# Where the new recurrent states are computed in the second feed-forward, and how its chunk borders are ordered

## The chip, the cores and the metric

The kernel runs on one core of a Trainium2 chip. The metric is the device time of one execution in microseconds (us), lower is better. Engines are named as in the profile: PE is the matrix engine (PEld its weight load), DVE the vector engine, ACT the scalar engine, POOL the GpSimd engine (here it mostly issues DMAs), SP the sync engine, which issues the other DMAs. Each engine works through its own instructions in the order in which they stand; semaphores make one engine wait for another.

## The reference

One layer of a decoder for 512 new prompt tokens and 8 single tokens that continue older sequences, all in float32. Norms, scales and the other outputs are left out here.

```python
def _swiglu(x, wg, wu, wd):
    return (jax.nn.silu(x @ wg) * (x @ wu)) @ wd
...
h = h + 0.5 * _swiglu(_rms_norm(h, ffn1_norm[l]), ffn1_w_gate[l], ffn1_w_up[l], ffn1_w_down[l])
m, p, c, s = _hybrid_mixer(_rms_norm(h, mix_norm[l]), ...)
h = h + m
h = h + 0.5 * _swiglu(_rms_norm(h, ffn2_norm[l]), ffn2_w_gate[l], ffn2_w_up[l], ffn2_w_down[l])
...
# in the mixer, for each of the 8 continued sequences:
def step(h, inp):
    s, a = inp
    return a[..., None, None] * h + s, h
```

D_MODEL is 1024 and FFN_DIM 2816. The last piece gives, for each continued sequence, 16 heads and a 64 x 128 matrix per head, a new state: the old state times a decay plus the outer product of two short vectors. These new states are an output of their own (`nss`, 8 x 1024 x 128 numbers); nothing else in the kernel reads them.

## The kernel before

The tokens lie along the free dimension, 520 of them in two halves of 260, the features along the 128 partitions. A float32 product is made of three matmuls on rounded parts, `hi*hi + hi*lo + lo*hi` (`mm3`, lines 123 to 128), so each operand is split: ACT rounds it to `hi`, DVE computes `lo = x - hi`. For some weight pieces `lo` is made by ACT, which writes the negative of the rounded value, and by a DMA of POOL that adds the original onto it (lines 111 and 112).

The kernel has three stages: the first feed-forward, the mixer, the second feed-forward. Both feed-forwards are the class `Ffn`. Its hidden features are 22 tiles of 128, in chunks of 6, 6, 6 and 4 (`CHUNKS`). A tile `f` is one step, and after each of the first three chunks four more steps `(c, d)` with d = 0, 2, 4, 6 multiply what chunk c has made by the down weights and add it to `h`. Between them, the first tile of the next chunk is already stepped: the order at a border is last tile of the chunk, first tile of the next, then `(c, 0)`, `(c, 2)`, `(c, 4)`, `(c, 6)`. I call this place a chunk border; there are three in each feed-forward.

A step multiplies two pairs of blocks with seven products instead of eight (Strassen's scheme): `product(k, p)` for p in 1, 5, 6, 3, 7, 2, 4, where p = 4 is left for the step after (`flush`). Each p reads one of seven "slots", which are the two halves of the left and the right member of a pair of tiles and sums and differences of them. For the `(c, d)` steps these slots are made of the activations: `g_split` (lines 252 to 294) makes, from the pair's tiles `gx` and `out`, four combinations `xd`, and rounds and subtracts all seven into the tile `gt` (seven `hi`, seven `lo`). Product 1 reads slot 0, 5 reads slot 3, 6 slot 5, 3 slot 2, 7 slot 4, 2 slot 1, 4 slot 6. For a chunk's last pair a part is made early (`g_split(k, False)` from `gates`) and the rest when product 4 is done (`g_split(k, True)` from `close`). In the first feed-forward (`self.i == 1`) the last pair of a chunk is already treated in its own way: the third combination is computed from other inputs, slot 3 is rounded apart from slots 4 and 5, the gate's instructions get high priority (`first_if`), and the weights of product 4 are split after the others (`late` in `load`).

The new states are a generator, `new_states` (lines 1001 to 1043), which the second feed-forward advances: 32 units, each one sequence and two pairs of heads. A unit is advanced twice. The first advance issues on POOL the store of the previous unit's result (`out_nss`, line 1021) and the load of the next unit's old state (`hs`, line 1011; three buffers), and for every second unit a load of a row (`br`, line 1017). The second advance issues four ACT instructions (lines 1037 and 1038) and one DVE addition (`hs`, line 1039). All but the DVE addition are pinned to the program's order. Before, `step` advances the generator twice per step (lines 526 and 527), that is, one unit per step in every step until the 32 are done.

The instructions of each engine are put in order by a scheduler that simulates the program's time with costs of its own; the diff therefore moves instructions that it doesn't name.

Of the kernel before, what the change touches and what calls it, by code (L numbers as in the profile page):

```python
# [12 lines left out]
ALU = mybir.AluOpType  # L13
# [21 lines left out]
PAIRED = 3  # L35
# [26 lines left out]
def tile_trunk_step(ctx: ExitStack, tc: tile.TileContext, ins: dict, outs: dict):  # L62
    nc = tc.nc
# [38 lines left out]
    def split(src, n, name, hp, nb, tags, late=None):  # L102
        hi, lo = (hp.tile([P, 1024], F32R, tag=t, bufs=nb, name=f"{t}_{name}")[:, :n] for t in tags)
        h, l = hi, lo
        if len(src.shape) == 3:
            h, l = (t.rearrange("p (j c) -> p j c", j=src.shape[1]) for t in (hi, lo))
        cast = nc.scalar.copy(h, src)  # L107
        casts.append(cast.ins)
        q = 0 if late is None else n - late.shape[1]
        if late is not None:  # L110
            nc.scalar.activation(out=lo[:, q:], in_=src[:, q:], func=AF.Copy, scale=-1.0)
            nc.gpsimd.dma_start(out=lo[:, q:], in_=late, accum_op=ALU.add)
        if late is None or q:
            s = slice(0, q) if late is not None else slice(None)
            nc.vector.tensor_tensor(out=l[:, s], in0=src[:, s], in1=h[:, s].bitcast(F32), op=ALU.subtract)
        return hi, lo
# [92 lines left out]
    class Ffn:  # L209
# [42 lines left out]
        def g_split(self, f, late=None):  # L252
            role = self.role(f)
            if role == "plain" and late is not False:
                self.g_plain(f, self.out[f])
            if role != "second":
                return
            last = f == self.chunks[self.chunk[f]][-1]
            if not last and late is False:
                return  # L260
            gx, go = self.gx, self.out[f]
            if not last or late is not True:
                self.gt[f] = (self.gp.tile([P, 14, HB], F32R, tag="gt", bufs=3, name=f"gt{self.i}_{f}"),
                              self.gp.tile([P, 4, HB], F32, tag="xd", name=f"gd{self.i}_{f}"))
            t, xd = self.gt[f]

            def low(x, q):
                hi, lo = t[:, 0:7][:, q], t[:, 7:14][:, q]
                nc.scalar.copy(hi, x)
                nc.vector.tensor_tensor(out=lo, in0=x, in1=hi.bitcast(F32), op=ALU.subtract)  # L270

            if not last or late is not True:
                nc.vector.tensor_tensor(out=xd[:, 0], in0=gx[:, 0], in1=gx[:, 1], op=ALU.subtract)
                nc.vector.tensor_tensor(out=xd[:, 1], in0=go[:, 1], in1=gx[:, 1], op=ALU.subtract)
                x, y = (xd[:, 0], go[:, 1]) if self.i == 1 else (xd[:, 1], gx[:, 0])
                nc.vector.scalar_tensor_tensor(out=xd[:, 2], in0=x, scalar=-1.0, in1=y, op0=ALU.mult, op1=ALU.subtract)
                low(gx[:, 0], 0)
                if last:
                    if self.i == 1:
                        low(xd[:, 0], 3)  # L280
                        low(xd[:, 1:3], slice(4, 6))
                    else:
                        low(xd[:, 0:3], slice(3, 6))
                    low(go[:, 1], 2)
            if last and late is False:
                return
            nc.vector.scalar_tensor_tensor(out=xd[:, 3], in0=xd[:, 2], scalar=-1.0, in1=go[:, 0], op0=ALU.mult,
                                           op1=ALU.subtract)
            if last:
                low(go[:, 0], 1)  # L290
                low(xd[:, 3], 6)
            else:
                low(go, slice(1, 3))
                low(xd, slice(3, 7))
# [101 lines left out]
        def load(self, k):  # L396
            wx = self.wx
            n, src, nb, raw, f1, f2, add = self.added.pop(k) if k in self.added else self.sums(k)
            d1 = split(raw[:, 0, : 2 * nb], 2 * nb, f"{n}a", wp, 3, ("whi", "wlo"), src[0, :, nb:])
            if add is not None:  # L400
                add()
            late = self.i == 1
            if not late:
                d2 = split(raw[:, 1, nb : 2 * nb], nb, f"{n}b", wp, 3, ("whi", "wlo"), src[1, :, nb:])
            e1 = split(f1, 2 * nb, f"{n}c", wx, 2, ("shi", "slo"))
            e2 = split(f2, 2 * nb, f"{n}d", wx, 2, ("shi", "slo"))
            if late:
                with tc.issue_after(casts[-1]):
                    d2 = split(raw[:, 1, nb : 2 * nb], nb, f"{n}b", wp, 3, ("whi", "wlo"), src[1, :, nb:])
            m = nb // P  # L410
            self.w[k] = {1: (d1, 0), 2: (d1, m), 7: (e1, 0), 5: (e1, m), 6: (e2, 0), 3: (e2, m), 4: (d2, 0)}
# [60 lines left out]

        def first_if(self, k):
            c = self.chunk[k]
            return tc.high_priority() if self.i == 1 and c < PAIRED and k == self.chunks[c][-1] else nullcontext()

        def up(self, k, b, u):
            out, tg = self.out[k][:, b], self.tg[k][:, b]
# [20 lines left out]
        def rest(self, before, last_chunk):  # L499
            for c, fs in enumerate(self.chunks):  # L500
                last = c == len(self.chunks) - 1
                for f in fs[self.direct if c == 0 else 1 :] + ([] if last else self.chunks[c + 1][:1]):
                    self.step(f)
                    if last and self.gx is not None:
                        self.g_plain(fs[0], self.gx)
                        self.gx = None
                if not last:
                    for d in range(0, KD, 2):
                        self.step((c, d))
            self.product(self.pending, 4)  # L510
            with tc.high_priority():
                self.close(self.pending)
            wd = before()
            if wd is not None:
                self.down_by_half(c, min(fs), last_chunk, wd)
            else:
                self.down(c, min(fs), KF, last_chunk)

        def step(self, k):
            if k not in self.A:  # L520
                self.product(k, 1)
            self.flush()
            for p in (2, 5, 6, 3, 7) if k == KF - 1 else (5, 6, 3, 7, 2):
                self.product(k, p)
                if p == 3:
                    self.state()
            self.state()
            self.gates(k)
            self.pending = k

        def state(self):
            if self.states is not None:
                next(self.states, None)

        def down(self, c, lo, hi, after):
# [171 lines left out]
    todo, late = [], []  # L707
# [607 lines left out]
```

## Time and profile before

| | us |
|---|---|
| median of 3 runs | 978.83 |
| the 3 runs | 979.16, 973.38, 978.83 |
| the profiled execution, its own time | 969.87 |
| its span in the trace | 968.1 |

The profiled execution is 8.96 us below the median of the runs shown, and 1.77 us longer than its span. In this profile a matmul's start and the next one's start are about 0.12 us apart when nothing holds PE up, while each one's record is 0.28 us long, since matmuls overlap. An idle time printed in brackets counts from the end of the matmul before, so the time lost is read from the starts.

The stages of the second feed-forward, by what PE works on: the first chunk from 621 us, its border from about 670 to 692, the second border from 772 to 785, the third from 865 to 878, the last tiles from about 903 to 936, then the down products of the last chunk and the final norm.

### The profile page before, as it was taken

Reading aid. Unit: us, or ns where it says so; the run is one execution under the profiler, and the core shown is the slowest. Engines: PE = TensorE matmul, PEld = TensorE weight load, DVE = VectorE, ACT = ScalarE, POOL = GpSimd, SP = SyncE. Lnnn points to the kernel's source line nnn. Section 1 sums busy time; section 2 is a strip of 40 time slices with the busy share of each in tenths; the row PEclk is TensorE's granted clock in tenths of the full one; section 3 lists DMA queues with packets and bytes.
Section 4 is the critical chain, followed back from the end, with each engine's and each line's share of the span. In section 5 each row is a group of like instructions: output and inputs, shape, how many; then the busy total and the mean of one; then the engine's idle time right before and its main releaser. Section 6 shows DMA issues by size and latency. Waiting matters only on the chain.

```text
span 968.1 us, 20281 instructions
## 1 busy us (share of the span) xinstructions
PE 941.7 (97%) x7636; PEld 921.6 (95%) x7636; DVE 858.1 (89%) x1613; ACT 693.5 (72%) x1290; POOL 234.8 (24%) x341
## 2 busy tenths in 40 slices
PE   7999999999999999999999999999999999999995
PEld 6999999999999999989899999899999999999995
DVE  7999899989999698688989876999999999999876
ACT  8777667667767475686776556678788888887864
POOL 0111211121122000156523111123332333333300
PEclk9999999999999999999999999999999999999998
DMA  7575775675666243254697776467687679767732
GB/s 243 152 173 125 174 178 125 148 188 148 156 150 169 67 151 119 87 186 124 166 255 219 176 178 153 120 155 185 144 228 199 151 176 233 169 167 185 189 88 89
DMA packets 66739, 157.01 MB, mean 162 GB/s; under 512 B 9608, under 2 KB 22856, under 8 KB 66640
## 3 DMA queue, kind: packets, MB, share of 16 engines
q1 hardware_dynamic: 41168, 103.78, 33.8%
q0 software_dynamic: 25472, 51.92, 29.3%
q8 instruction: 60, 0.98, 0.4%
q14 instruction: 39, 0.32, 0.1%
HBM read 148.33 MB, written 7.34 MB: 161 GB/s over the span
## 4 chain that ended last, share of the span: by engine, by line
PE 85%; DVE 7%; DMA 3%; ACT 2%; issue 2%; SPq 0%; POOL 0%; DVEq 0%; ACTq 0%
PE A L128 8%; PE A L124 8%; PE A L127 8%; PE BE L124 6%; PE BE L127 6%; PE BE L128 6%; PE P L320 3%; PE wo L124 2%; PE wo L128 2%; PE wo L127 2%; PE inz L124 2%; DMA raw<-in_w1gu 2%; PE A2d L127 2%; PE A2d L128 2%; PE A2d L124 2%
## 5 line engine op out<-in xcount | busy, mean ns | idle before, releaser
L447 ACT COPY ac<-A 128x260 f32<-128x260 f32 x123 | 45.3, 369 | 15.4 <-PE A L128 15.1
L390 DVE TENSOR_TENSOR s<-raw 128x1024 f32<-128x1024 f32 x41 | 50.0, 1220 | 3.1 <-DMA raw<-in_w1gu 2.1
L1021 POOL DMA_DIRECT2D out_nss<-hs x32 | 20.7, 646 | 83.3 <-DVE hs L1039 73.9
L124 PE MATMUL inz<-xh_mx,whi_inz 128*128 128x260 f32 x128 | 36.8, 288 | 1.0 <-DVE E L1115 1.0
L124 PE MATMUL wo<-catg,whi_wo 128*128 128x260 f32 x128 | 37.2, 291 | 0.0
L320 PE MATMUL P<-xg_f,raw 128*128 128x260 f32 x128 | 31.7, 400 | 5.4 <-DMA raw<-in_w1gu 5.4
L124 PE MATMUL inx<-xh_mx,whi_inx 128*128 128x260 f32 x128 | 36.5, 285 | 0.0
L128 PE MATMUL wo<-catg,wlo_wo 128*128 128x260 f32 x128 | 36.3, 283 | 0.0
L128 PE MATMUL inz<-xh_mx,wlo_inz 128*128 128x260 f32 x128 | 36.2, 283 | 0.0
L128 PE MATMUL inx<-xh_mx,wlo_inx 128*128 128x260 f32 x128 | 36.2, 283 | 0.0
L127 PE MATMUL inx<-xl_mx,whi_inx 128*128 128x260 f32 x128 | 36.2, 283 | 0.0
L127 PE MATMUL wo<-catg,whi_wo 128*128 128x260 f32 x128 | 36.2, 283 | 0.0
L127 PE MATMUL inz<-xl_mx,whi_inz 128*128 128x260 f32 x128 | 36.2, 283 | 0.0
L320 PEld LDWEIGHTS P<-xg_f,raw 128*128 128x128 f32 x128 | 25.1, 200 | 9.1 <-ACT xg_f L193 5.3
L885 DVE SCALAR_TENSOR_TENSOR A<-U,h,A 128x544 f32<-128x544 f32 x36 | 28.2, 782 | 5.1 <-ACT A L883 4.8
L459 DVE TENSOR_TENSOR tg<-BE,ac 128x520 f32<-128x520 f32 x41 | 28.6, 697 | 4.5 <-PE BE L128 4.5
L1139 DVE TENSOR_TENSOR h<-wo,h 128x260 f32<-128x260 f32 x48 | 19.6, 424 | 12.5 <-PE wo L128 12.5
L469 DVE TENSOR_TENSOR tg<-tg,r_f 128x520 f32<-128x520 f32 x41 | 28.7, 701 | 2.2 <-ACT tg L467 2.1
L991 DVE SCALAR_TENSOR_TENSOR junk<-h,cb 128x128 f32<-128x128 f32 x64 | 21.8, 340 | 9.6 <-DMA cb<-scr_bc 8.7
L107 ACT CAST whi_wo<-raw_wo 128x1024 fp32r<-128x1024 f32 x12 | 12.6, 1047 | 23.6 <-issue 15.6
L467 ACT ACTIVATE tg<-tg 128x520 f32<-128x520 f32 x41 | 26.2, 639 | 3.6 <-DVE tg L466 3.6
L466 DVE TENSOR_TENSOR tg<-tg,r_f 128x520 f32<-128x520 f32 x41 | 28.6, 699 | 0.1
(1803 smaller groups left out, 4820.7 us busy)
## 6 DMA issues: line engine op xcount, KB each, us to landing
raw<-in_w2gu SPq DMA_DIRECT2D x44, 512.0 KB, 5.1
raw<-in_w1gu SPq DMA_DIRECT2D x42, 512.0 KB, 4.7
raw_1d<-in_w1d SPq DMA_DIRECT2D x24, 384.0 KB, 3.9
raw_2d<-in_w2d SPq DMA_DIRECT2D x24, 384.0 KB, 4.0
raw_wo<-in_w_out SPq DMA_DIRECT2D x12, 512.0 KB, 6.6
wlo_wo<-in_w_out POOLq DMA_DIRECT2D x12, 512.0 KB, 7.9
ab<-scr_acs SPq DMA_DIRECT2D x8, 512.0 KB, 5.1
h<-in_state_ssm SPq DMA_DIRECT2D x16, 256.0 KB, 6.8
```

Source lines behind the costliest of these rows:

```text
L124: first = nc.tensor.matmul(ps, whi, xhi, start=start, stop=False, **kw)
L127: nc.tensor.matmul(ps, whi, xlo, start=False, stop=False, **kw)
L128: nc.tensor.matmul(ps, wlo, xhi, start=False, stop=stop, **kw)
L320: nc.tensor.matmul(self.banks[f, u][b][:, :HB], ws(self.raw[f][:, u], j + 4 * q), xg[:, slot[q]], start=j == q == 0, stop=j == 3 and q == ...
L390: nc.vector.tensor_tensor(out=s1, in0=diag, in1=up0, op=ALU.add)
L447: nc.scalar.copy(keep, out[:, :HB])
L459: nc.vector.tensor_tensor(out=tg, in0=self.BE[k][:, :, :HB], in1=a, op=ALU.add)
L466: nc.vector.tensor_tensor(out=tg, in0=tg, in1=r, op=ALU.mult)
L467: nc.scalar.activation(out=tg, in_=tg, func=AF.Silu)
L469: nc.vector.tensor_tensor(out=tg, in0=tg, in1=r, op=ALU.mult)
L885: nc.vector.scalar_tensor_tensor(out=A[:, :n], in0=U[:, j : j + n], scalar=w(j), in1=A[:, :n], op0=ALU.mult, op1=ALU.add)
L991: nc.vector.scalar_tensor_tensor(out=junk, in0=h0[:, q], scalar=1.0, in1=cb, op0=ALU.mult, op1=ALU.mult, accum_out=ysm[:, 4 * g + q, b : b ...
```

## The change

Four edits, all of which act in the second feed-forward alone.

1. `g_split`: for a chunk's last pair the second feed-forward now does what the first already did. The third combination is computed from `xd[:, 0]` and `go[:, 1]`, and slot 3 is rounded and subtracted (260 columns) apart from slots 4 and 5 (520 columns), where one pair of instructions over 780 columns did it.
2. `load`: for the steps `(c, 2)` the weights of product 4 are split after the other weights.
3. `first_if`: the high priority holds in the second feed-forward too.
4. `step` and `state`: no unit is advanced in the last tile's step of the first three chunks, nor in `(c, 0)` and `(c, 2)`, nine steps in all. In the steps of the last chunk's four tiles (18 to 21) the generator is advanced after each of the five products and once more, six times, so three units per step. What is left is drained after the loop. Tile 18 belongs to the last chunk, but its step stands at the third border.

```diff
-                x, y = (xd[:, 0], go[:, 1]) if self.i == 1 else (xd[:, 1], gx[:, 0])
-                nc.vector.scalar_tensor_tensor(out=xd[:, 2], in0=x, scalar=-1.0, in1=y, op0=ALU.mult, op1=ALU.subtract)
+                nc.vector.scalar_tensor_tensor(out=xd[:, 2], in0=xd[:, 0], scalar=-1.0, in1=go[:, 1], op0=ALU.mult,
+                                               op1=ALU.subtract)
                 low(gx[:, 0], 0)
                 if last:
-                    if self.i == 1:
-                        low(xd[:, 0], 3)
-                        low(xd[:, 1:3], slice(4, 6))
-                    else:
-                        low(xd[:, 0:3], slice(3, 6))
+                    low(xd[:, 0], 3)
+                    low(xd[:, 1:3], slice(4, 6))
                     low(go[:, 1], 2)
...
-            late = self.i == 1
+            late = self.i == 1 or isinstance(k, tuple) and k[1] == 2
...
-            return tc.high_priority() if self.i == 1 and c < PAIRED and k == self.chunks[c][-1] else nullcontext()
+            return tc.high_priority() if c < PAIRED and k == self.chunks[c][-1] else nullcontext()
...
+            for _ in self.states or ():
+                pass
             self.product(self.pending, 4)
...
                 self.product(k, p)
-                if p == 3:
-                    self.state()
-            self.state()
+                if p == 3 or self.catch_up(k):
+                    self.state(k)
+            self.state(k)
...
-        def state(self):
-            if self.states is not None:
+        def catch_up(self, k):
+            return not isinstance(k, tuple) and self.chunk[k] >= PAIRED
+
+        def at_border(self, k):
+            if isinstance(k, tuple):
+                return k[1] in (0, 2)
+            return self.chunk[k] < PAIRED and k == self.chunks[self.chunk[k]][-1]
+
+        def state(self, k):
+            if self.states is not None and not self.at_border(k):
                 next(self.states, None)
```

Nothing moves ahead of the second feed-forward. In it, three places are shown, each as the rows stand on one engine; a row has the line, the operation, what it writes and reads and the size, and the long numbers at a name's end are buffer numbers.

On DVE at the second border, before (`gt_11` and `gd_11` are the slots and combinations of the last pair of that chunk, tile 12 is the next chunk's first, `2d_1` the down weights):

```order
L270 TENSOR_TENSOR gt_11_10040<-tg_11_10034,gt_11_10040 128x260
L276 SCALAR_TENSOR_TENSOR gd_11_10041<-gd_11_10041,gx_8_9901 128x260
L466 TENSOR_TENSOR tg_12_10188<-tg_12_10188,r_f_7641 128x520
L115 TENSOR_TENSOR slo_2d_1d<-s_2d_1_10199,shi_2d_1d 128x768
L449 TENSOR_TENSOR ac_12_1_10081<-ac_12_1_10081 128x260
L1039 TENSOR_TENSOR hs_10000<-hs_10000,so_10182 128x256
L287 SCALAR_TENSOR_TENSOR gd_11_10041<-gd_11_10041,tg_11_10034 128x260
L270 TENSOR_TENSOR gt_11_10040<-gd_11_10041,gt_11_10040 128x780
```

The same place of the change, in two pieces, the first from a little earlier in the program:

```order
L273 TENSOR_TENSOR gd_11_10003<-gx_8_9872 128x260
L270 TENSOR_TENSOR gt_11_10002<-gx_8_9872,gt_11_10002 128x260
L387 TENSOR_TENSOR s_2d_1_10162<-raw_2d_1_10159 128x768
L115 TENSOR_TENSOR slo_12d<-s_2_12_10019,shi_12d 128x1024
L446 TENSOR_TENSOR ac_11_1_9905<-ac_11_1_9905 128x260
L463 TENSOR_TENSOR tg_11_9996<-tg_11_9996,r_f_7641 128x520
L270 TENSOR_TENSOR gt_11_10002<-gd_11_10003,gt_11_10002 128x260
```

```order
L463 TENSOR_TENSOR tg_12_10152<-tg_12_10152,r_f_7641 128x520
L115 TENSOR_TENSOR slo_2d_1d<-s_2d_1_10163,shi_2d_1d 128x768
L284 SCALAR_TENSOR_TENSOR gd_11_10003<-gd_11_10003,tg_11_9996 128x260
L446 TENSOR_TENSOR ac_12_1_10045<-ac_12_1_10045 128x260
L1046 TENSOR_TENSOR hs_9834<-hs_9834,so_10146 128x256
L270 TENSOR_TENSOR gt_11_10002<-gd_11_10003,gt_11_10002 128x520
```

The 780 columns that stood at the end of the piece are 260 columns (slot 3) 19 rows earlier and 520 columns at the old place, still behind the addition `hs` of tile 12's unit. The unit of tile 11's step, which stood between the two pieces, is gone from there.

On ACT at the third border, before, from the copy after tile 18's product 7:

```order
L447 COPY ac_18_1_11402<-A_18_11399 128x260
L1037 ACTIVATE hs_11321<-hs_11321,sdec 128x128
L1038 ACTIVATE so_11503<-br_11184,sxdt 128x128
L1037 ACTIVATE hs_11321<-hs_11321,sdec 128x128
L1038 ACTIVATE so_11503<-br_11184,sxdt 128x128
L447 COPY ac2d_2_0_11545<-A2d_2_11543 128x260
L269 CAST gt_17_11361<-gd_17_11362 128x780
L467 ACTIVATE tg_18_11509<-tg_18_11509 128x520
L107 CAST whi_2d_2a<-raw_2d_2_11632 128x768
L111 ACTIVATE wlo_2d_2a<-raw_2d_2_11632 128x384
L269 CAST gt_17_11361<-gd_17_11362 128x260
L447 COPY ac2d_2_1_11546<-BE2d_2_11544 128x260
```

and in the change, from the same copy (another unit begins ten rows above it):

```order
L444 COPY ac_18_1_11339<-A_18_11336 128x260
L1044 ACTIVATE hs_11385<-hs_11385,sdec 128x128
L1045 ACTIVATE so_11437<-br_11128,sxdt 128x128
L1044 ACTIVATE hs_11385<-hs_11385,sdec 128x128
L1045 ACTIVATE so_11437<-br_11128,sxdt 128x128
L444 COPY ac2d_2_0_11500<-A2d_2_11498 128x260
L269 CAST gt_17_11296<-gd_17_11297 128x520
L444 COPY ac2d_2_1_11501<-BE2d_2_11499 128x260
L107 CAST whi_2d_2a<-raw_2d_2_11578 128x768
L111 ACTIVATE wlo_2d_2a<-raw_2d_2_11578 128x384
L464 ACTIVATE tg_18_11464<-tg_18_11464 128x520
L1044 ACTIVATE hs_11419<-hs_11419,sdec 128x128
```

The copy `ac2d_2_1` now stands right behind the cast of the slots, ahead of the weights; three units stand around tile 18's step.

On ACT at the end of the second feed-forward, before, from the last tile's second copy to the rounding of the last activations:

```order
L447 COPY ac_21_0_12276<-A_21_12274 128x260
L107 CAST shi_2d_3_12413<-raw_2d_3_12411 128x512
L107 CAST shi_2d_3_12418<-raw_2d_3_12411 128x512
L447 COPY ac_21_1_12277<-A_21_12274 128x260
L467 ACTIVATE tg_21_12372<-tg_21_12372 128x520
L576 CAST dhi_2d_3_12424<-raw_2d_3_12422 128x512
```

and in the change:

```order
L444 COPY ac_21_0_12255<-A_21_12253 128x260
L107 CAST shi_2d_3_12419<-raw_2d_3_12417 128x512
L1044 ACTIVATE hs_12212<-hs_12212,sdec 128x128
L1045 ACTIVATE so_12316<-br_12177,sxdt 128x128
L1044 ACTIVATE hs_12212<-hs_12212,sdec 128x128
L1045 ACTIVATE so_12316<-br_12177,sxdt 128x128
L464 ACTIVATE tg_21_12377<-tg_21_12377 128x520
L107 CAST shi_2d_3_12424<-raw_2d_3_12417 128x512
L444 COPY ac_21_1_12256<-A_21_12253 128x260
L1044 ACTIVATE hs_12299<-hs_12299,sdec 128x128
L1045 ACTIVATE so_12350<-br_12301,sxdt 128x128
L1044 ACTIVATE hs_12299<-hs_12299,sdec 128x128
```

From the rounding of tile 18's activations (`gt_18`) on, ACT has nine units where it had two, and the last of them stands between two casts of the last down weights.

## The prediction

> **What bounds the kernel now.** I read the page first, then the busy times by stretch, then PE's waits, then single instructions where PE stood still.
>
> ```profile
> span 968.1 us, 20281 instructions
> PE 941.7 (97%) x7636; PEld 921.6 (95%) x7636; DVE 858.1 (89%) x1613; ACT 693.5 (72%) x1290; POOL 234.8 (24%) x341
> PE 85%; DVE 7%; DMA 3%; ACT 2%; issue 2%; SPq 0%; POOL 0%; DVEq 0%; ACTq 0%
> ```
>
> PE is busy for 97% of the span and makes 85% of the chain that ended last. The change takes no matmul away, so all that it can win is time in which PE stands still in the second feed-forward, and all that it can lose is new time of that kind. The stretches of that stage (length, then the busy time of PE, PEld, DVE, ACT and POOL) show how much there is:
>
> ```profile
> 621.00:670.00 49.00, 46.51 (x374) 45.24 (x373) 47.39 (x75) 37.77 (x73) 12.29 (x19) 1.00 0.65 165
> 670.00:692.00 22.00, 21.02 (x172) 20.41 (x171) 21.71 (x42) 17.45 (x38) 7.17 (x10) 1.00 0.65 154
> 692.00:772.00 80.00, 80.00 (x667) 80.00 (x666) 76.08 (x125) 66.40 (x136) 26.24 (x38) 1.00 0.78 193
> 772.00:785.00 13.00, 11.85 (x96) 11.43 (x95) 12.88 (x27) 9.99 (x23) 5.40 (x8) 1.00 0.66 152
> 785.00:865.00 80.00, 80.00 (x668) 80.00 (x668) 76.05 (x125) 66.66 (x137) 26.58 (x38) 1.00 0.77 190
> 865.00:878.00 13.00, 11.86 (x97) 11.44 (x95) 12.68 (x25) 9.99 (x23) 4.98 (x8) 1.00 0.66 155
> 905.00:940.00 35.00, 34.99 (x291) 34.78 (x290) 27.87 (x47) 22.85 (x45) 5.76 (x8) 1.00 0.52 136
> ```
>
> Between the borders PE never stops. It is idle for 0.98, 1.15 and 1.14 us at the three borders, 3.27 us in all, 2.49 us in the first tiles, which the change hardly touches, and 0.01 us in the stretch of the last tiles. The borders are where DVE is full (12.88 of 13 us); the last tiles are where DVE and ACT have the most room (7.1 and 12.2 us of 35).
>
> **What a border costs.** PE at the third border:
>
> ```profile
> 872.85 0.28 PE L124 MATMUL A2d<-gt,shi_2d_2d 128*128 128x260 f32 x1
> 873.99 0.39 PE L127 MATMUL BE2d<-gt,shi_2d_2c 128*128 128x260 f32 x1 [0.86 <-DVE gt L270]
> 874.34 0.28 PE L127 MATMUL A2d<-gt,shi_2d_2d 128*128 128x260 f32 x1
> 874.46 0.28 PE L128 MATMUL A2d<-gt,slo_2d_2d 128*128 128x260 f32 x1
> 875.02 0.39 PE L124 MATMUL BE2d<-gt,shi_2d_2d 128*128 128x260 f32 x1 [0.28 <-ACT ac2d L447]
> ```
>
> Undisturbed starts lie 0.12 us apart, so the two gaps lose 1.14 - 0.12 = 1.02 and 0.56 - 0.12 = 0.44 us: 1.46 us, 0.32 more than the 1.14 us of the stretch, 0.16 for each gap. The second border has the same idle time, 1.47 us by the same rule. At the first, the idle time lies in two gaps too, both behind ACT copies:
>
> ```profile
> PE BE2d L124 <- ACT ac2d L447: 0.7, 1, 0.7
> PE BE L124 <- ACT ac L447: 0.3, 1, 0.3
> ```
>
> 0.98 + 0.32 = 1.30 us. Together the borders cost 1.30 + 1.47 + 1.46 = 4.23 us. The first gap of the later two waits for DVE's 780-column subtraction; this is what DVE does just ahead of it at the second border:
>
> ```profile
> 779.38 0.43 DVE L449 TENSOR_TENSOR ac<-ac 128x260 f32<-128x260 f32 x1
> 779.72 0.42 DVE L1039 TENSOR_TENSOR hs<-hs,so 128x256 f32<-128x256 f32 x1
> 780.05 0.43 DVE L287 SCALAR_TENSOR_TENSOR gd<-gd,tg 128x260 f32<-128x260 f32 x1
> 780.39 0.97 DVE L270 TENSOR_TENSOR gt<-gd,gt 128x780 fp32r<-128x780 f32 x1
> 781.27 0.56 DVE L391 TENSOR_TENSOR s_2d<-s_2d,raw_2d 128x384 f32<-128x384 f32 x1
> ```
>
> By their starts the unit's addition holds DVE 0.33 us, 260 columns 0.34 us and 780 columns 0.88 us.
>
> **Slot 3 apart, and the gates first.** Product 5, the second of a border step, needs slot 3 alone, but gets it with slots 4 and 5 in one instruction that starts when the third combination is there. In the new order slot 3 is done 19 DVE rows earlier, before the last tile's gate, and product 6's share of the last pair (slot 5) stands behind products 3 and 2. So the 1.02 us gap should go; the next that is late is slot 5, and PE has some 20 matmuls (2.4 us) more to do before it. The copy behind which the second gap waits now stands right behind the slots' cast on ACT instead of behind the weights. The price is one ACT and one DVE instruction more at each border: 260 columns cost 0.34 and 780 cost 0.88, which gives 0.27 per 260 and 0.07 fixed, 0.07 us three times, 0.2 us of DVE, at a place where it has none to spare.
>
> [...]
>
> What does the same arrangement cost where it already runs? The first feed-forward has it, without any states, and its three borders show two waits of PE and none at the third:
>
> ```profile
> PE A1d L128 <- DVE slo_1d_0d L115: 0.4, 1, 0.4
> PE A1d L128 <- DVE slo_1d_1d L115: 0.2, 1, 0.2
> ```
>
> With 0.16 per gap that is 0.56, 0.36 and 0 us, 0.92 in all. I take this as what remains. The bounds are 0 and 4.23.
>
> **Late weights of `(c, 2)`.**
>
> ```profile
> 876.34 0.83 ACT L107 CAST shi_2d_2c<-s_2d 128x768 fp32r<-128x768 f32 x1 [1.09 <-PE BE2d L127]
> wlo_2d_2b<-in_w2d POOLq DMA_DIRECT2D x4, 192.0 KB, 6.4
> ```
>
> This moves one cast, one negation and one POOL DMA of three steps behind two casts of 0.83 us on ACT; POOL's queue keeps its order, since its next state DMAs are gone there. The DMA takes 6.4 us to land, and product 4 reads it about a step of 63 matmuls (7.6 us) later. I cost it at nothing; if that cover fails, it is at most the two casts, 1.7 us a step.
>
> **Units off the borders.** A unit's ACT part:
>
> ```profile
> 902.62 0.40 ACT L1037 ACTIVATE hs<-hs,sdec 128x128 f32<-128x128 f32 x1
> 902.92 0.39 ACT L1038 ACTIVATE so<-br,sxdt 128x128 f32<-128x128 f32 x1
> 903.21 0.39 ACT L1037 ACTIVATE hs<-hs,sdec 128x128 f32<-128x128 f32 x1
> 903.50 0.39 ACT L1038 ACTIVATE so<-br,sxdt 128x128 f32<-128x128 f32 x1
> 903.80 0.36 ACT L447 COPY ac<-A 128x260 f32<-128x260 f32 x1
> ```
>
> By starts 1.18 us of ACT, and 0.33 us of DVE. At the first two borders one unit stays, that of the next chunk's first tile. At the third, tile 18 counts as of the last chunk, so its step gets three units in the place where three stood in tiles 17, 18 and the first `(c, d)` step: this border is not relieved of them, only closer packed. Beyond the 0.92 us I add 0.3 us there, one DVE addition; bounds 0 and the whole 1.46. The borders then win 4.23 - 0.92 - 0.3 = 3.0 us.
>
> **Units in the last chunk.** From tile 18's rounding on ACT has nine units instead of two, most of them in the 35 us from 905. Seven more are 8.3 us of ACT, which has 12.2 idle there, and 2.3 us of DVE, which has 7.1: 89% and 86% busy. Between the borders ACT runs at 83% and DVE at 95% with PE never waiting; at a border, with DVE at 99%, PE loses 1.46 us in 13. So the price lies between 0 and 1.46 x 35/13 = 3.9 us, nearer the first; below nothing it can't go, since PE has 0.01 us to win there. I take 0.8 us, because ACT is in order and a unit stands ahead of copies on which PE waits: that after tile 21's product 7 ended 0.8 us before PE's next matmul on that bank.
>
> ```profile
> 933.29 0.37 ACT L447 COPY ac<-A 128x260 f32<-128x260 f32 x1
> 934.48 0.28 PE L124 MATMUL A<-xth_f,whi_21b 128*128 128x260 f32 x1
> ```
>
> On POOL the stores and loads of these units stand ahead of tile 21's weights, and each store waits for its unit on DVE:
>
> ```profile
> POOL out_nss L1021 <- DVE hs L1039: 73.9, 22, 5.1
> 917.09 0.85 POOL L112 DMA_DIRECT2D wlo_21a<-in_w2gu  x1 [1.73 <-ACT wlo_21a L111]
> DMA to landing us min/median/max: 3.7/3.7/3.7
> L128 PE MATMUL BE<-xth_f,wlo_21a x8: 277/282/286, 319.3 to 923.7; 128*128 128x260 f32 x8
> ```
>
> The first of tile 21's added pieces lands at 917.09 + 3.7 = 920.8, and PE's last matmul on it starts at 923.7, the first nine starts (1.1 us) before: 1.8 us of cover for POOL, so nothing is charged. The last stores come behind the last unit, still ahead of the output's.
>
> **The sum.** -3.0 + 0.8 = -2.2 us: the profiled execution's 969.87 becomes 967.7, and the median of 978.83 becomes **976.6**. The three runs spread over 5.8 us, more than the whole effect; about 1% (9.8 us) is what I take a measurement of this kernel to tell from no change.
>
> **Rivals.**
> *DVE stays the bound of the borders.* It runs at 99% there, loses one 0.33 us addition at the border proper and gains 0.07; the wait would move on to slot 5 or to the next weights, and only some 0.3 us a border would be won. For it: the fill of DVE. Against it: the first feed-forward's borders, and the 20 matmuls put in front of slot 5. -1 + 0.8: 978.6.
> *The last chunk takes it back.* ACT's order holds PE as DVE does at a border: -3.0 + 3.9, 979.7. For it: nine units among the copies; against it: 12.2 us of idle ACT.
> *The three state buffers run short, which is slower.* A buffer is loaded, computed on, stored and freed.
>
> ```profile
> L1011 POOL DMA_DIRECT2D hs<-in_state_ssm x32: 556/564/891, 620.4 to 906.3; - x32
> DMA to landing us min/median/max: 2.0/2.9/6.9
> DMA to landing us min/median/max: 2.0/2.7/6.7
> ```
>
> The second line is the load's, the third the store's. By the medians the round is 2.9 + 1.18 + 0.42 + 2.7 + 2 x 0.56 = 8.3 us, 2.8 per unit with three buffers; the last chunk asks for one every 3.4 us (84 matmuls of 0.12 us a step, three units). At the greatest landings it is 16.3 us, 5.4 per unit, and then 12 units pull ACT, and with it PE, by 12 x 2.0 = 24 us; halfway, 12 us: 978.83 - 3.0 + 12 = 988 and up. It decides from a mean landing of about 3.7 us. Against it: the DMA engines are less loaded there (0.52) than between borders (0.78). [...]
> *It doesn't do what it says.* At the third border it doesn't, by the order; that is in the sum.
>
> **Numbers.** Forecast 0.62, DVE stays the bound 0.20, the last chunk takes it back 0.11, buffers 0.07. Faster by over 1% can't come from the trace: all idle time of PE from 621 to 940 is 2.49 + 3.27 + 0.01 = 5.8 us. Only run spread could add to it: 0.05. Slower by over 1%: most of the buffers' case, 0.06. Range: from a gain of 4 us met by runs as low as the lowest shown (5.4 us under the median), about 970, to the third case with some 2 us more of the buffers' one, 982.
>
> **What would show it.** Right: PE's waits at 780 and 873 us on `gt` gone or below 0.4 us, no wait of PE in the last tiles above 0.5 us, their ACT near 31 of 35 us. Wrong: PE waiting there for ACT copies, ACT waiting for the load of `hs`, or waits at the borders under another name.

## The result and the profile after

| | before | changed |
|---|---|---|
| median, us | 976.70 (22 runs) | 972.38 (22 runs) |
| lowest and highest, us | 968.70, 980.32 | 968.93, 977.11 |
| the profiled execution, us | 969.87 | 970.42 |
| ratio of times | | 0.9964 (95%: 0.9947 to 0.9982) |

The timed difference is a third of a per cent, within what counts as no change. The two profiled executions differ by 0.55 us the other way. Which of the two describes the change is the first question, and the stretches answer it in part. The head of the page, and the stretches of the prediction's table that touch the change, of the changed kernel:

```profile
span 968.7 us, 20265 instructions
PE 942.4 (97%) x7636; PEld 922.2 (95%) x7636; DVE 859.2 (89%) x1616; ACT 694.3 (72%) x1293; POOL 232.1 (24%) x341
```

```profile
670.00:692.00 22.00, 22.00 (x185) 22.00 (x184) 21.12 (x40) 16.41 (x34) 4.63 (x6) 1.00 0.55 128
772.00:785.00 13.00, 12.65 (x105) 12.44 (x104) 12.46 (x27) 10.17 (x23) 2.62 (x3) 1.00 0.55 133
865.00:878.00 13.00, 12.20 (x101) 11.99 (x100) 12.50 (x27) 12.42 (x31) 5.44 (x8) 1.00 0.62 143
905.00:940.00 35.00, 34.99 (x291) 34.77 (x290) 30.34 (x54) 31.01 (x74) 15.07 (x25) 1.00 0.73 186
```

The last row is as forecast: ACT works 31.01 of 35 us with the additional units, and PE still never stops. DVE has some room at the borders now (12.46 and 12.50 of 13 us). PE's idle time there isn't gone, though, and the first row only looks so because the wait of the first border now falls behind 692 us. PE's waits in the second feed-forward:

```profile
PE A L124 <- ACT ac L444: 1.5, 3, 0.5
PE BE L124 <- ACT ac L444: 1.4, 2, 1.0
PE BE2d L124 <- ACT shi_2d_0c L107: 0.9, 1, 0.9
PE BE2d L124 <- ACT shi_2d_1c L107: 0.9, 1, 0.9
PE BE2d L124 <- ACT shi_2d_2c L107: 0.8, 1, 0.8
```

No wait on `gt` is left. In its place there is one wait at each border, on ACT's cast of weights, `shi` of the step `(c, 2)`. At the second border, DVE, then ACT, then PE:

```profile
781.91 0.69 DVE L270 TENSOR_TENSOR gt<-gd,gt 128x520 fp32r<-128x520 f32 x1
784.62 0.83 ACT L107 CAST shi_2d_1c<-s_2d 128x768 fp32r<-128x768 f32 x1 [1.59 <-PE A2d L127]
784.25 0.28 PE L127 MATMUL A2d<-gt,shi_2d_1d 128*128 128x260 f32 x1
784.37 0.28 PE L128 MATMUL A2d<-gt,slo_2d_1d 128*128 128x260 f32 x1
785.50 0.39 PE L124 MATMUL BE2d<-gt,shi_2d_1c 128*128 128x260 f32 x1 [0.86 <-ACT shi_2d_1c L107]
```

Slots 4 and 5 are finished at 782.6 us. The last two matmuls of product 6, which read slot 5 of the last pair, stand behind products 3 and 2 on PE and run only at 784.25 and 784.37 us. They are the last readers of the buffer into which the weights of the step `(c, 2)` are cast: ACT stood idle for 1.59 us waiting for them, PE then waits for ACT, and the gap between starts is 1.14 us (1.13 by the rounded rows), 1.02 us lost. It is the size of the wait on `gt` that went at the later two borders.

**A measure that doesn't carry the spread.** The four matmuls on `psr_f` end PE's part of the norm ahead of the second feed-forward, the two on `psl` end PE's work. Their starts in the kernel before, in a second execution of the kernel before (a run below), and in the changed kernel:

```profile
620.67 1.04 PE L171 MATMUL psr_f<-acc_f,ones 128*128 128x260 f32 x4
957.81 0.71 PE L733 MATMUL psl<-sq_last,ones 128*128 128x260 f32 x2 [0.24 <-ACT sq_last L717]
```

```profile
629.47 1.04 PE L171 MATMUL psr_f<-acc_f,ones 128*128 128x260 f32 x4
966.66 0.71 PE L733 MATMUL psl<-sq_last,ones 128*128 128x260 f32 x2 [0.24 <-ACT sq_last L717]
```

```profile
621.56 1.04 PE L171 MATMUL psr_f<-acc_f,ones 128*128 128x260 f32 x4
958.37 0.71 PE L740 MATMUL psl<-sq_last,ones 128*128 128x260 f32 x2 [0.24 <-ACT sq_last L724]
```

From the one to the other it is 337.14 and 337.19 us before and 336.81 us after. The two executions of the kernel before differ by 8.84 us in time, and by 0.05 us in this stretch: what spreads lies ahead of it. The experiments are read by this length, from the last of the `psr_f` matmuls to PE's last (0.33 us less than by these rows), and by PE's lost time in it. That is the sum of all gaps between starts longer than 0.16 us, each less 0.12 us; shorter gaps are left out, so that lost times explain differences of length to about 0.3 us only. By the length the change wins 0.4 us:

| us | first 56 us | border 1 | border 2 | border 3 | between borders | length |
|---|---|---|---|---|---|---|
| before | 4.21 | 1.76 | 1.73 | 1.73 | 0 | 336.81 |
| before, second execution | 4.22 | 1.77 | 1.72 | 1.72 | 0 | 336.86 |
| changed | 5.31 | 1.16 | 1.16 | 1.07 | 0.18 | 336.47 |
| changed, second execution | 5.25 | 1.16 | 1.16 | 1.11 | 0.18 | 336.44 |
| border arrangement alone | 5.28 | 1.74 | 2.03 | 1.73 | 0.72 | 339.11 |
| states alone | 4.25 | 1.63 | 1.23 | 2.28 | 0 | 336.91 |
| combination as before but in last pairs | 4.26 | 1.66 | 1.12 | 2.71 | 0 | 337.37 |
| without late weights | 5.23 | 1.14 | 1.14 | 1.77 | 0.37 | 337.37 |
| product 2 first in `(c, 2)` | 5.25 | 5.87 | 2.21 | 4.47 | 0.39 | 347.56 |
| both of these (combination, product 2) | 4.26 | 5.33 | 2.12 | 3.10 | 0 | 342.44 |
| product 5 behind product 7 | 5.33 | 1.40 | 1.40 | 1.34 | 0.82 | 337.94 |
| the same, combination as before but in last pairs | 4.26 | 1.94 | 1.40 | 2.75 | 0 | 338.05 |
| product 2 behind product 6 | 5.28 | 0.83 | 0.79 | 0.97 | 0.18 | 335.62 |
| changed, without units | 2.89 | 1.43 | 1.16 | 1.12 | 0 | 334.15 |

The borders are counted from 56 to 110, 155 to 180 and 250 to 275 us of the stretch. What is left is the last tiles and the end, 1.96 us in all rows but two (3.62 with product 2 first in `(c, 2)`, 2.06 in the second run with product 5 behind product 7). Each row is one traced execution, and only the kernel before and the changed one were traced twice.

### The profile page after: what moved, and what is told of

Same layout as the page of the kernel before. It is cut to its first block, busy times and chain, and to the rows that moved or that the text cites. A ratio compares the mean times of both kernels' runs of the same rounds, so it can differ in the third digit from the quotient of the medians.

```text
span 968.7 us, 20265 instructions
## 1 busy us (share of the span) xinstructions
PE 942.4 (97%) x7636; PEld 922.2 (95%) x7636; DVE 859.2 (89%) x1616; ACT 694.3 (72%) x1293; POOL 232.1 (24%) x341
## 4 chain that ended last, share of the span: by engine, by line
PE 86%; DVE 6%; DMA 3%; ACT 3%; issue 2%; POOL 0%; SPq 0%; DVEq 0%; ACTq 0%
PE A L128 8%; PE A L124 8%; PE A L127 8%; PE BE L128 6%; PE BE L124 6%; PE BE L127 6%; PE P L317 3%; PE wo L124 2%; PE wo L128 2%; PE wo L127 2%; PE A2d L127 2%; PE A2d L124 2%; PE A2d L128 2%; PE inz L124 2%; PE A1d L128 2%
```

## The experiments

**The two kernels once more.** Unchanged copies.

> The kernel before against itself: 1.000, with an interval that says what 5 rounds tell apart, I expect 0.002 either way. Its trace should show the same three waits on gt and ac; places whose lost time differs from the first trace by more than 0.3 us vary from run to run whatever the change does.

> The changed kernel once more, for its size and a second trace. If the ratio of 0.9964 is real: 0.995 to 0.998, about 3.5 us faster. If it came from which runs happened to be drawn, as the two profiled executions suggest (970.42 against 969.87 us): 0.999 to 1.001. In the trace the first product of the steps (c, 2) waits about 1.0 us for the cast of shi at each border if the wait belongs to the order; the extra 1.5 us that PE lost in the first tiles, about 658 us, come again if they belong to the change, and not if they are a late DMA of that one execution.

Measured: before against itself 1.0008 (0.9986 to 1.0031), changed 0.9999 (0.9973 to 1.0025). In this set the change is worth nothing that can be timed, and the first set's 0.9964 didn't come again. In the traces it came again to 0.03 us: length 336.44, the same three waits for `shi`, and 5.25 us lost in the first tiles, so that loss belongs to the change. What spreads is seen in the second execution of the kernel before, 8.84 us longer. It falls behind in the mixer, 6.9 us of it around one place, where PE waits 4.39 us for a DVE that itself waits for a DMA; the last section shows what else happens there.

```profile
543.16 0.29 DVE L991 SCALAR_TENSOR_TENSOR junk<-h,cb 128x128 f32<-128x128 f32 x1 [7.56 <-DMA cb<-scr_bc]
544.12 1.23 PE L171 MATMUL psr_y<-X,ones 128*128 128x260 f32 x2 [4.39 <-DVE E L1115]
```

**One half of the change at a time.** First the borders' arrangement, with units as before:

```diff
-                if p == 3 or self.catch_up(k):
+                if p == 3:
...
-            if self.states is not None and not self.at_border(k):
+            if self.states is not None:
```

> Slot 3 apart, the gates first and the late weights; the states advance one unit in every step as before. If the borders' arrangement brings the gain: 0.996 to 0.998. If the gain comes from the states leaving the borders: 0.999 to 1.001, and DVE's addition of a unit still in front of slots 4 and 5. If the new wait for the cast of shi comes from the late slot 5: PE waits for shi here too, 0.8 to 1.0 us at the later two borders.

Then the units' places alone, with the other three edits undone (two of the places are shown):

```diff
-                    low(xd[:, 0], 3)
-                    low(xd[:, 1:3], slice(4, 6))
+                    if self.i == 1:
+                        low(xd[:, 0], 3)
+                        low(xd[:, 1:3], slice(4, 6))
+                    else:
+                        low(xd[:, 0:3], slice(3, 6))
...
-            late = self.i == 1 or isinstance(k, tuple) and k[1] == 2
+            late = self.i == 1
```

> The states leave the borders and go into the last chunk, with the borders' code as before. If the states bring the gain: 0.996 to 0.998, and the wait of PE for the 780 columns of gt shrinks by a unit's DVE addition, from 1.02 to 0.7 us. If the arrangement does: 0.999 to 1.001, and the wait on gt stays at 1.0 us, because product 5 still needs the subtraction over 780 columns. If the last chunk costs anything (0.8 us in the forecast, 3.9 at most), it is seen here: up to 1.003.

Measured: 1.0013 (0.9984 to 1.0043) and 1.0009 (0.9984 to 1.0033), which tell nothing apart; the traces do. The arrangement alone is 2.3 us longer than before. It has the waits for `shi` in full and a further 0.51 us at each border behind an ACT copy (the first row). The states alone are 0.1 us longer, hardly more than two executions differ by; their waits on `gt` stay (the other rows), 0.4 us lost at the second border and 1.2 at the third, where tile 18's step has three units and which is worse than before:

```profile
PE A2d L124 <- ACT ac2d L444: 1.0, 3, 0.3
```

```profile
PE BE2d L127 <- DVE gt L270: 1.3, 2, 1.0
PE BE2d L124 <- ACT ac2d L447: 1.3, 3, 0.7
```

Neither expectation of one part "bringing the gain" held: at the borders and between them the arrangement alone loses 1.0 us, the states alone win 0.08, and together they win 1.65 (5.22 to 3.57). So each needs the other here.

**The first tiles.** The line above `if last:` is executed for every pair of tiles, not only for a chunk's last; the list of edits speaks of last pairs alone. Here it is kept for those:

```diff
-                nc.vector.scalar_tensor_tensor(out=xd[:, 2], in0=xd[:, 0], scalar=-1.0, in1=go[:, 1], ...)
+                x, y = (xd[:, 0], go[:, 1]) if self.i == 1 or last else (xd[:, 1], gx[:, 0])
+                nc.vector.scalar_tensor_tensor(out=xd[:, 2], in0=x, scalar=-1.0, in1=y, ...)
```

> The third combination is computed the new way for a chunk's last pair alone; for the other pairs as before. Read by the length from the last matmul on psr_f to PE's last matmul (before 336.81 and 336.86 us in two executions, the change 336.47 and 336.44) and by PE's lost time in the first 56 us of it (4.21 and 4.22 before, 5.31 and 5.25 with the change). If the new inputs of the combination in the pairs that are not last reorder ACT and DVE there: the lost time falls back to 4.2 and the length to 335.4. If the border's own edits reach back into the first tiles: 5.3 and 336.5. The wait for the cast of shi stays, 1.0 us at each border.

Measured: 4.26 us lost in the first tiles, so it is this line; two later runs that have it this way lose 4.26 us there too. The length didn't follow: 337.37. At the third border the scheduler now puts product 4 of `(2, 0)` ahead of product 1 of `(2, 2)`, and 0.82 and 0.63 us more are lost behind ACT copies there; the first border gives back 0.5 of what it had won. The two new waits:

```profile
PE A2d L124 <- ACT ac2d L444: 1.1, 2, 0.7
```

In the first tiles, ACT before (the first two rows) and after (the next two), and PE after:

```profile
653.25 1.05 ACT L107 CAST shi_2d<-s 128x1024 fp32r<-128x1024 f32 x1
654.47 0.40 ACT L1037 ACTIVATE hs<-hs,sdec 128x128 f32<-128x128 f32 x1
```

```profile
654.39 0.41 ACT L1044 ACTIVATE hs<-hs,sdec 128x128 f32<-128x128 f32 x1
655.58 1.03 ACT L107 CAST shi_2d<-s 128x1024 fp32r<-128x1024 f32 x1
659.01 0.39 PE L124 MATMUL BE<-xth_f,shi_2d 128*128 128x260 f32 x1 [0.38 <-ACT ac L444]
659.76 0.38 PE L128 MATMUL A<-xth_f,slo_2d 128*128 128x260 f32 x1 [0.25 <-DVE slo_2d L115]
```

The cast of tile 2's weights stood ahead of a unit and stands behind it now, 2.33 us later by these rows, of which 0.89 us are the later start of the whole stretch. PE's wait for `slo_2d` follows from it, since DVE makes `slo_2d` from this cast; the other wait is for an ACT copy that also comes later in the new order.

**Late weights.** Undone for `(c, 2)`:

```diff
-            late = self.i == 1 or isinstance(k, tuple) and k[1] == 2
+            late = self.i == 1
```

> The change without its late weights in the steps (c, 2). If the late weights cost nothing, as forecast: length 336.4 to 336.6 with them or without. If they are what keeps the cast of shi from being later still: without them the wait for shi grows by a cast and a negation, 0.8 to 1.3 us at each border, length up to 340. If they delay something: shorter than 336.3.

Measured: length 337.37, 0.9 us longer, so the late weights don't merely cost nothing, they win. The wait for `shi` grows at the third border alone; at the others the negation takes its place:

```profile
PE BE2d L124 <- ACT shi_2d_2c L107: 1.5, 1, 1.5
PE A2d L124 <- ACT wlo_2d_1b L111: 0.7, 1, 0.7
PE A2d L124 <- ACT wlo_2d_0b L111: 0.7, 1, 0.7
```

**Filling the gap with product 2 of the next step.**

```diff
-            for p in (2, 5, 6, 3, 7) if k == KF - 1 else (5, 6, 3, 7, 2):
+            for p in (2, 5, 6, 3, 7) if k == KF - 1 or self.i == 2 and isinstance(k, tuple) and k[1] == 2 else (5, 6, 3, 7, 2):
```

> The steps (c, 2) begin with product 2, which needs weights that lie ready, so that product 5 stands about 8 matmuls later. If the wait at the borders is one for the buffer of shi, which product 6's late last pair gives back late: it falls from 1.0 us to 0.1 to 0.3 at each border, and the length from 336.45 to about 334.0. If it is the ACT queue that makes the cast late, or if the next thing is late right behind it: the wait stays at 0.8 or more, or moves on to the sums or weights that come next, and the length stays above 336.

> xd2_last and p2first in one kernel. If both causes are as stated: lost time 4.2 in the first tiles and about 0.3 at each border, length 333 to 333.5, 3.4 us less than before, ratio 0.9965. If the waits only move on: 336 and a ratio of 1.000. Neither can be told from the timed rounds alone when their interval is 0.0025 wide either way.

Measured: length 347.56 and 342.44, and 1.0068 (1.0039 to 1.0097) for the two edits together, slower than before. The wait for `shi` is gone in both; so far the reading held. What came next was worse, weights that a DMA of POOL completes:

```profile
PE BE2d L128 <- DMA wlo_2d_0a<-in_w2d: 3.0, 1, 3.0
PE BE2d L128 <- DMA wlo_2d_2a<-in_w2d: 1.9, 1, 1.9
PE BE2d L128 <- DMA wlo_2d_1a<-in_w2d: 1.8, 1, 1.8
```

These are the waits with product 2 alone moved. "Weights that lie ready" was wrong: their `hi` half does, their `lo` half doesn't. The three waits are 6.7 of the 11 us by which this run is longer than the changed kernel; where most of the rest went stands in the last section.

**Filling it with product 7 of the same step.**

```diff
+            if p == 7:
+                self.seven = end.ins
...
-                self.product(k, p)
+                with tc.issue_after(self.seven) if self.i == 2 and isinstance(k, tuple) and k[1] == 2 and p == 5 else nullcontext():
+                    self.product(k, p)
```

> The change with one order fixed on PE: product 5 of the steps (c, 2) stands behind product 7 of (c, 0), 9 matmuls (1.08 us) later; no other product moves, and the weights are split as in the change. If the wait at the borders is one for the buffer of shi, given back by product 6's late last pair: the cast ends about 0.1 us before PE comes to product 5, the wait of 1.0 us is gone at all three borders, and the length from the last matmul on psr_f to PE's last falls from 336.45 to about 333.5. If slots 4 for product 7, or weights of (c, 2), are as late as the cast was: a wait of about the same size under another name, length 336 or more. Ratio by the first 0.9965, by the second 0.9995.

> The same, and the third combination computed the new way for a chunk's last pair alone. If the two act apart: 4.2 us lost in the first tiles instead of 5.3, no wait for shi, length 332.5 to 333. If the order that the scheduler then makes at the third border (product 4 ahead of product 1 of the next step, which lost 0.82 and 0.63 us there in the run without the fixed order) costs what it cost: 1.1 less in the first tiles, 0.5 more at the first border, 1.6 more at the third, length about 334.5.

Measured: length 337.94 and 338.05; 1.0029 (1.0000 to 1.0058) and 1.0005 (0.9977 to 1.0034). The second theory held in its size, but the wait is neither for slot 4 nor for weights: it is for the copy of bank `A`. Product 7 adds into the bank that product 6 has filled, and ACT must copy it out in between. ACT, and PE, at the second border with product 5 behind product 7:

```profile
788.00 0.83 ACT L107 CAST shi_2d_1c<-s_2d 128x768 fp32r<-128x768 f32 x1 [1.61 <-PE A2d L127]
788.74 0.37 ACT L446 COPY ac2d<-A2d 128x260 f32<-128x260 f32 x1
789.16 0.39 PE L124 MATMUL A2d<-gt,shi_2d_1c 128*128 128x260 f32 x1 [1.13 <-ACT ac2d L446]
```

The cast for which PE had waited and this copy both start from the end of product 6, one behind the other. So whatever PE does next must need neither.

**Product 2 of `(c, 0)` behind product 6's last pair.** It is a product at this place that needs neither; in the changed kernel it stands just ahead.

```diff
+            if p == 6:
+                self.six = end.ins
...
-                self.product(k, p)
+                with tc.issue_after(self.six) if self.i == 2 and isinstance(k, tuple) and k[1] == 0 and p == 2 else nullcontext():
+                    self.product(k, p)
```

> The change with product 2 of the steps (c, 0) fixed behind product 6's late last pair on PE, so that 9 matmuls (1.08 us) lie between that pair and the first product that needs something ACT makes from it. If the last pair's end is the cause, since it starts both the cast of shi (0.83 us) and the copy of A (0.37 us) that come next on ACT: the borders lose 0.1 to 0.5 us each instead of 1.1, the length from the last matmul on psr_f to PE's last falls from 336.45 to 334.2 to 335. If slot 5 comes too late for the earlier place: a wait on gt of 0.3 us or more there. If the wait moves on once more: 336 to 337 and a name not seen so far. Ratio 0.997 to 0.999 by the first.

Measured: length 335.62, 0.84 us less than the changed kernel and 1.2 less than before, the shortest that computes everything; timed 1.0001 (0.9970 to 1.0033), which can't show 0.1%. The wait for `shi` is gone at the first two borders:

```profile
PE BE2d L124 <- ACT ac2d L446: 1.0, 2, 0.5
PE BE2d L124 <- ACT shi_2d_2c L107: 0.7, 1, 0.7
```

```profile
787.48 0.83 ACT L107 CAST shi_2d_1c<-s_2d 128x768 fp32r<-128x768 f32 x1 [0.49 <-PE A2d L127]
```

```profile
879.71 0.39 ACT L1048 ACTIVATE so<-br,sxdt 128x128 f32<-128x128 f32 x1
880.00 0.39 ACT L269 CAST gt<-gd 128x260 fp32r<-128x260 f32 x1
880.30 0.83 ACT L107 CAST shi_2d_2c<-s_2d 128x768 fp32r<-128x768 f32 x1
```

ACT's rows are of the second and the third border. At the second the cast starts while PE works on product 2's nine matmuls, and the next gap loses 0.04 us. The forecast of 0.1 to 0.5 us per border was missed (0.83, 0.79 and 0.97 us): behind an ACT copy 0.64 us come up some 4 us later, at product 3 of the next step. At the third, tile 18's unit stands on ACT ahead of the cast, which no longer waits for its buffer but for its turn.

**No units at all.** This kernel leaves one output out, the new states.

```diff
-            for _ in self.states or ():
-                pass
...
-            if self.states is not None and not self.at_border(k):
+            if False:
```

> The changed kernel with the 32 units left out: no new states are computed, loaded or stored. If the units that the change left at the borders or put into the last chunk still cost something: the length from the last matmul on psr_f to PE's last falls by 0.5 us or more below 336.45. If after the change the borders hang on the buffer of shi alone: a wait of 1.0 us for its cast stays at the later two borders, where PE's order is the change's own, they lose 1.1 us each, and the length is 335.5 to 336.5, the rest being what the scheduler makes of the first tiles. If the loss of 1.1 us in the first tiles comes from the units there: 4.2 us lost in the first 56 us instead of 5.3.

Its stretch of the first 56 us, with the same stretch of the kernel before and of the changed one below it, and its waits:

```profile
625.90:681.90 56.00, 54.59 (x444) 53.61 (x443) 55.19 (x85) 39.55 (x69) 7.79 (x9) 1.00 0.59 149
```

```profile
621.30:677.30 56.00, 53.51 (x432) 52.27 (x431) 54.41 (x86) 43.95 (x87) 13.66 (x20) 1.00 0.67 169
```

```profile
622.20:678.20 56.00, 52.89 (x424) 51.27 (x423) 54.40 (x85) 42.42 (x82) 13.70 (x20) 1.00 0.62 158
```

```profile
PE BE2d L124 <- ACT shi_2d_1c L107: 0.9, 1, 0.9
PE BE2d L124 <- ACT shi_2d_0c L107: 0.9, 1, 0.9
PE BE2d L124 <- ACT shi_2d_2c L107: 0.9, 1, 0.9
```

Measured: length 334.15. So the 32 units cost the changed kernel 2.3 us in all, and none of it at the borders, which lose as much without them: it lies in the first tiles, 2.4 us, to which the change adds no unit and from which it takes none but tile 5's. That is more than the 1.1 us that the change lost there, and it was never priced.

## Why the prediction held, and which of its steps did not

The median of 972.38 us lies inside the range, and no change that timing could tell was the likeliest case. That says little for the sum: the range was 12 us wide, for the spread of the runs, and the change's own size is 0.4 us by the traces instead of 2.2. The terms were off on both sides and made up for each other in part, which was luck. Of the prediction's signs of being right all three came (no wait on `gt`, none above 0.5 us in the last tiles, ACT at 31 us there), but so did one of being wrong, "waits at the borders under another name".

- *"The borders then win ... 3.0 us."* They won 1.65. Their loss before was 5.22 us by the table, not 4.23, mainly since the prediction left out that the start after the one that waited comes late too, 0.22 us behind it instead of 0.12. The wait for 780 columns went, as stated. What took its place was first seen in the trace after: product 6's late last pair gives a weight buffer back late, and the cast behind it is what PE waits for. Product 6 was priced only by when slot 5 is ready ("some 20 matmuls (2.4 us) more to do before it"); slot 5 was ready 1.6 us before PE used it. The term left out was what hangs on the end of that pair: its weight buffer and its bank. It is shown by the run with product 2 behind that pair, where the wait goes at the first two borders, and by the run without units, where it stays at all three.
- *"2.49 us in the first tiles, which the change hardly touches."* It lost 1.1 us there. The new inputs of the third combination hold for all pairs, which the list of edits overlooked; the run that keeps them to last pairs takes the loss away.
- *"I take 0.8 us"* for the last chunk. It cost nothing: PE 34.99 of 35 us, with ACT at 31.01. The buffers' rival fell too; ACT waits for the load of a state 0.2 us in all there.
- *"I cost it at nothing"* for the late weights: without them the kernel is 0.9 us longer, so their price was below nothing, an end that was not considered.
- *"I take this as what remains"*, 0.92 us from the first feed-forward's borders together, was no measure for the second, whose borders lose 1.1 to 1.4 us each even without units.
- The extra 0.3 us of the third border did not appear in the changed kernel (1.07 and 1.11 us, as the others); in the run with the states alone, the same three units made it the worst, 2.28.

Of the rivals, *DVE stays the bound of the borders* came nearest, "on to slot 5 or to the next weights": it was the next weights, and 0.55 us a border were won where it said some 0.3. Its reason, DVE's fill, was not it, since ACT and DVE both had done their part and ACT stood idle for 1.59 us. DVE was busy for 12.88 and 12.68 of 13 us at the later two borders before, and the wait on `gt` went all the same, with the arrangement alone too. The split of the 780 columns was not run apart from the other edits of that arrangement, so what it costs or wins by itself is not shown.

The timed ratio of the first set, 3.5 us by its middle and 1.8 by its nearer end, is more than the 0.4 us that the traces show, and it was 0.9999 when repeated. One execution of the kernel before was seen to fall 8.84 us behind in the mixer, ahead of anything the change moves. That the first set's difference came from such pauses is likely, but it was not shown.

## What to carry to other kernels

When a consumer is moved later to give its input time, list what its end releases (the buffers it reads last, the bank it fills) and look at who waits for those: at two borders a wait of 1.02 us on an input became one of 1.02 us on a buffer. When a profile's spread is larger than the effect, find two marks around the code that changed and compare that stretch, which here agreed to 0.05 us where times differed by 8.84. And filling a gap needs work whose every operand is ready, low halves from DMAs included.

## What the runs showed of the hardware

Behind some pauses of PE the granted clock was lower, and more time was lost than the pause itself. With product 2 first, PE waited 3.0 us at the first border, and for 6 us after it the granted clock was 0.50. Length, busy times and clock of that run around the first, second and third border:

```profile
701.00:704.00 3.00, 0.39 (x4) 0.18 (x2) 2.91 (x6) 1.11 (x2) 0.66 (x1) 0.90 0.45 66
704.00:710.00 6.00, 5.57 (x25) 5.57 (x26) 2.22 (x4) 1.48 (x4) 0.00 (x0) 0.50 0.00 0
801.00:805.00 4.00, 4.00 (x36) 4.00 (x35) 2.91 (x5) 2.51 (x5) 0.27 (x1) 1.00 0.00 0
894.50:898.00 3.50, 3.50 (x17) 3.50 (x18) 1.20 (x2) 0.00 (x0) 0.00 (x0) 0.51 0.04 13
```

25 records in 5.57 us of work are one start per 0.22 us instead of 0.12. Behind the pause of 1.8 us at the second border the clock was 1.00; the one of 1.9 us at the third was followed by 3.5 us at 0.51. In the run with product 2 first and the combination as before, the clock was 1.00 in the 3.5 us behind a pause of 2.5 us at the third border. So the length of a pause doesn't decide alone; what else does was not shown. The mixer's pause of 4.39 us, in the second execution of the kernel before, has a lower clock behind it too, 0.60 in the 5 us from 545 us:

```profile
545.00:550.00 5.00, 5.00 (x27) 5.00 (x27) 4.89 (x27) 0.48 (x1) 0.00 (x0) 0.60 0.76 174
```
